# SSD scan: the norms' transposes and root broadcasts written to the four PSUM banks of the outputs' pool

## Chip, cores and metric

The kernel runs on one core of one Trainium2 chip. The metric is the device time of one execution in microseconds (us). Three executions of the kernel before gave 2980.72, 2979.49 and 2980.98 us, median 2980.72.

## What is computed

One step of a two-layer encoder on 1024 prompt frames and 64 sample frames (1088 columns). Layer 0 is an SSD (Mamba-2) mixer and a feed-forward block, layer 1 a chunk-band attention and a feed-forward block. The change is in layer 0's mixer. Cut to what matters:

```python
z, xbc, dt_raw = split(u @ w_in)                  # u = rmsnorm(x)
xs, Bm, Cm = split(silu(conv(xbc)))
y, h_final = ssd_scan(xs, softplus(dt_raw + dt_bias), -exp(A_log), Bm, Cm, h0)
y = (y + xs * D_skip) * silu(z)                   # (L, 2048)
yg = y.reshape(L, 4, 512)                         # 4 groups
yg = yg * rsqrt(mean(yg * yg, -1) + EPS)          # a norm for each group and row
return (yg.reshape(L, 2048) * gnorm_w) @ w_out
```

## The kernel before

Data lie with features on the 128 partitions and the 1088 columns along the free axis, in three slices of 384, 384 and 320 columns (`SL`, numbered s = 0, 1, 2). Matmuls of weights run in three passes each (lines 454 to 456: high part by high, high by low, low by high). Every tile that TensorE writes stands in one of the eight PSUM banks. In the SSD stage two belong to the pool `pmm` (tag `mm`, the projections), two to `pax` (tag `ax`, called the shared ones here) and four to `pyy` (tag `yy`).

**The stage.** TensorE's program is written by hand: the loop of lines 1079 to 1101 issues one projection tile after another (`unit`), and after each quarter or half of one `st.pump()` lets side tasks add their pieces, by due times on a clock that the program keeps for itself (`Stream`). The side tasks are

- `group_task`: two tiles `bnp`, `cbp` a slice and group, from `ax`;
- `ssd_task` for each block j of 128 features (16 of them, four to a group) and slice: a transpose `xtp` (line 866), read by VectorE as `xd` (876), and a state product `sp` (885), read by VectorE as `hn` (898), both from `ax`;
- `ssd_out` (809), once for two (j, s): two tiles `yp` and two tiles `yo` from `pyy`, read by VectorE at lines 830 and 832;
- at the end of a group's last block, for each slice, `rstd` (482): three transposes of the sums of squares `ssg` into `nst` (line 487), a reduce of it on VectorE (498) and eight small steps (499 to 511) that give the inverse roots `rst`;
- `build_y` (581): takes the finished y back from DRAM (`yt`, line 596), and for one column quarter q and group broadcasts the roots over the partitions, by two or three transposes into `nbp` (`bcast`, 517), which ScalarE copies to `rb` (520). `rb` has one buffer. VectorE multiplies (597), ScalarE and VectorE split the product into its high and low part (598, 599). This is the right-hand side of the output projection (`project`).

Before the change both `nst` and `nbp` came from `ax`, through the function of line 436. With two banks, a tile of `ax` has to wait until the tile two before it, or the one before it, has been read. Groups 0 to 2 have their three norms in the middle of the stage; the norms of group 3 stand in its last 15 us, mixed with the first broadcasts of `build_y`. That end is called the tail here.

**Order.** TensorE executes the program's order. The order on the other engines comes from a scheduler with priorities; `rstd` and the projections' evacuations have the highest (`HIP`). For the last block (j = 15) the sums of squares are added on VectorE (line 933, `end = V`) in place of GpSimd. From line 1104 on, the first output projection (`project`) runs, and then the feed-forward stage, whose pool `px0` takes over the four banks of `pyy`.

The program prints names without numbers: `nst<-ident,ssg` is a norm's transposes of this stage, `nst<-ident,ssum` one of another stage.

Of the kernel before, what the change touches and what calls it, by code (L numbers as in the profile page):

```python
# [8 lines left out]
F32 = mybir.dt.float32  # L9
# [7 lines left out]
P = 128  # L17
# [357 lines left out]
def hybrid_kernel(  # L375
# [57 lines left out]
    def col(c):  # L433
        return pcs[:, c:c + 1]

    def ax(name):
        return pax.tile([P, 512], F32, tag="ax", name=name)

    def mm(name):
# [21 lines left out]
    def unit(w, u, n, evac, parts=2, pl=None):  # L461
        ps_ = mm("mm") if pl is None else pl.tile([P, 512], F32, tag="mm", name="mmx")
        passes(ps_, w, lambda k: u[k], [(k, k) for k in range(KD)], n, parts=parts)
        evac(ps_)
        st.pump()
# [16 lines left out]
    def rstd(ssum, inv, r, nb, more=None):  # L482

        sp = ax("nst")
        if more is None:
            for i in range(nb):
                PE.transpose(sp[:, i * P:(i + 1) * P], ssum[:, i * P:(i + 1) * P], ident)
        else:
            for j, t in enumerate((ssum, more)):
                for i in range(nb):  # L490
                    c = 4 * j + i
                    PE.matmul(sp[:, c:c + 1], t[:, i * P:(i + 1) * P], ones[:, 0:1], start=True, stop=True)
        with tc.high_priority(HIP):
            v = nsb.tile([P, 12], F32, tag="nv", bufs=2, name="nv")
            a, h, y = v[:, 0:nb], v[:, 4:4 + nb], v[:, 8:8 + nb]
            if more is None:
                sums = sp[:, :nb * P].rearrange("p (a b) -> p a b", b=P)
                V.tensor_reduce(a, sums, axis=mybir.AxisListType.X, op=ALU.add)
                V.tensor_scalar(a, a, inv, EPS, op0=ALU.mult, op1=ALU.add)
            else:  # L500
                V.tensor_scalar(a, sp[:, :nb], inv, EPS, op0=ALU.mult, op1=ALU.add)
                V.scalar_tensor_tensor(a, sp[:, 4:4 + nb], inv, a, op0=ALU.mult, op1=ALU.add)
            V.tensor_scalar(y.bitcast(I32), a.bitcast(I32), -0.5, float(0x5F3759DF), op0=ALU.mult, op1=ALU.add)


            V.tensor_tensor(h, y, y, op=ALU.mult)
            V.tensor_tensor(h, h, a, op=ALU.mult)
            V.scalar_tensor_tensor(a, h, RP[0], h, op0=ALU.add, op1=ALU.mult)
            V.scalar_tensor_tensor(a, a, RP[1], h, op0=ALU.add, op1=ALU.mult)
            V.scalar_tensor_tensor(a, a, RP[2], h, op0=ALU.add, op1=ALU.mult)  # L510
            V.scalar_tensor_tensor(r, a, RP[3], y, op0=ALU.add, op1=ALU.mult)

    def bcast(r, a, n, rb=None):

        bp = ax("nbp")
        for i in range((a + n + P - 1) // P):
            PE.transpose(bp[:, i * P:(i + 1) * P], r[:, i:i + 1].to_broadcast([P, P]), ident)
        if rb is None:
            rb = nsb.tile([P, 384], F32, tag="rb", bufs=1, name="rb")
        A.activation(rb[:, :n], bp[:, a:a + n], AF.Copy, scale=RL)  # L520
        return rb[:, :n]
# [82 lines left out]
    def project(qs, uq, y, src, after=None, early=None, pl=None):  # L604


        ss = {}
        for mg in MGS:
            ws = early if early and mg is MGS[0] else [W.get() for _ in mg]
            for q in qs:  # L610
                n = QS[q][1]
                st.wait_for(lambda: q in uq)
                for m, w_ in zip(mg, ws):
                    ym = y[q][m // 4][:, m % 4, :]

                    def ev(ps):
                        with tc.high_priority(HIP):
                            if src is None:
                                A.copy(ym, ps[:, :n])
                            else:  # L620
                                V.tensor_tensor(ym, src[q][m // 4][:, m % 4, :], ps[:, :n], op=ALU.add)

                    if not (ws is early and q == qs[0]):
                        unit(w_, uq[q], n, ev, pl=pl)
                    if after:
                        if m == 0:
                            ss[q] = ssum_start(n)
                        add_sq(ss[q], ym, n, m == 0)
                    if q == qs[-1]:
                        W.put()  # L630
                if mg is MGS[-1]:
                    R.put(4)
                    if src is not None and src is not y:
                        R.put(2)
                    if after:
                        after(q, ss[q])

    with ExitStack() as es:
        pyy = es.enter_context(tc.tile_pool(reuse_waits="tile", name="pyy", bufs=4, space=PSUM))
# [34 lines left out]

        def table_task():
            ps = ax("dtn")
            for c in range(NCH):
                PE.matmul(ps[:, c * 32:(c + 1) * 32], dtT[c // 3][:64, (c % 3) * P:(c % 3 + 1) * P], stk, start=True, stop=True)
# [263 lines left out]
        def evac_of(kind, i):  # L942
            if kind == "z":
                def f(s, p_):
                    n = SL[s][1]
                    zst[i, s] = sb2.tile([P, 384], F32, tag="zs", bufs=3, name="zs")
                    scaled(zst[i, s][:, :n], p_, s, 0, n)
                    A.activation(zst[i, s][:, :n], zst[i, s][:, :n], AF.Silu)
                    if i == 15:
                        drop_u(s)  # L950
                        if s == 0:
                            st.spawn(build_y())
                return f
            if kind == "x":
                cvx = pair_t[i] = Conv(i, "xsT", 5)

                def f(s, p_):
                    cvx(s, p_)
                    st.spawn(ssd_task(i, s))
                return f  # L960
            if kind == "B":
                grp_t[i] = Conv(16 + i, "BT", 2), Conv(20 + i, "CT", 5)
                return grp_t[i][0]
            cvc = grp_t[i][1]

            def f(s, p_):
                cvc(s, p_)
                st.spawn(group_task(i, s), SSD_D)
            return f
# [71 lines left out]
        def scale_dt(s):  # L1041
            st.wait_for(lambda: s in done)
            ps = pend[s].pop(0)
            V.tensor_tensor(dtT[s][:64, :SL[s][1]], ps[:64, :SL[s][1]], rbs[s][:64, :SL[s][1]], op=ALU.mult)

        def finish(s):
            if s < 1:
                scale_dt(s)
            for e, ps in zip(ev, pend.pop(s)):
                e(s, ps)  # L1050

        for s in range(NSL):
# [23 lines left out]
                dps = dt_unit(us, n, pl, tg)  # L1076
            pend[s] = [dps] * (s < 2) + box
        finish(2)
        for grp in order:
            ws = [W.get() for _ in grp]  # L1080
            ev = [evac_of(*f) for f in grp]
            if len(grp) < 3:
                seq = [(i, s) for s in range(NSL) for i in range(len(grp))]
                if grp is order[0]:

                    seq = [(0, 0), (0, 1), (1, 0), (1, 1), (1, 2), (0, 2)]
            else:
                seq = [(0, 0), (1, 0), (0, 1), (0, 2), (2, 0), (1, 1), (2, 1), (1, 2), (2, 2)]
            for i, s in seq:
                kd_, jj_ = grp[i]  # L1090
                q = 3 * jj_ + s
                if kd_ == "x":
                    st.wait_for(lambda: so["C"] > q - 5)
                elif kd_ == "z":
                    st.wait_for(lambda: so["D"] > q - 3)
                elif kd_ == "C" and q >= 5:
                    g_, s_ = divmod(q - 5, 3)
                    st.wait_for(lambda: so["C"] > 3 * (4 * g_ + 3) + s_)
                unit(ws[i], u[s], SL[s][1], lambda p_: ev[i](s, p_))
                if s == 2:  # L1100
                    W.put()
# [5 lines left out]
            ya[q] = [v4(R.get(), QS[q][1]) for _ in range(2)]  # L1107
        project((0, 1), uy[0], ya, None)
        st.wait_for(lambda: so["D"] == 3 * XT and len(rst_done) == NG * NSL)


    class Ops:
# [889 lines left out]
```

## Time and profile before

| | |
|---|---|
| median of three executions | 2980.72 us |
| profiled execution | 2979.66 us, of which the span of its instructions is 2978.0 us |
| TensorE busy | 2921.0 us, 98% of the span |
| VectorE / ScalarE / GpSimd busy | 69% / 47% / 24% |
| SSD stage with group norms (200 to 640 us) | TensorE busy 434.56 of 440 us, VectorE 360.01 |
| tail (656 to 671 us) | TensorE busy 11.29 of 15 us, VectorE 15.00 |
| mean granted TensorE clock | 0.996 |

Times in the rows are us from the span's start. A row of the timeline has start, length, engine, line, operation, out<-in, shape and count, and in brackets how long the engine had been idle before it and what ended that. PE is TensorE's matmuls, DVE VectorE, ACT ScalarE, POOL GpSimd, SP the queue that issues DMAs. A matmul's end is modelled, and matmuls overlap: three transposes in a row are shown as 0.49 us, but the next instruction starts 0.32 us after the first of them. What one instruction costs the stream is therefore read from start to start. Each row of the waits says who waited for whom, the sum, how many times, and the longest.

### The profile page before, as it was taken

What the parts mean: (1) busy time and instruction counts of PE and PEld (TensorE: products, weight loads), DVE (VectorE), ACT (ScalarE), POOL (GpSimd) and SP (SyncE); (2) the same over time, 40 slices, a digit from 0 to 9 for tenths busy, and PEclk for the clock granted to TensorE, in tenths of its full rate; (3) what the DMA queues carried; (4) which work ended last, traced back from release to release, by engine and by line L of the source; (5) the groups of instructions that cost most, each with busy time, mean ns of one, the idle gap of its engine ahead of it and who ended that gap; (6) DMA issues with size and microseconds to landing.
All of it is one profiled execution on the core that took longest, in us unless ns stands there. A gap on an engine that the chain in (4) does not pass through costs nothing.

```text
span 2978.0 us, 56302 instructions
## 1 busy us (share of the span) xinstructions
PE 2921.0 (98%) x21626; PEld 2871.4 (96%) x21626; DVE 2040.2 (69%) x4471; ACT 1394.1 (47%) x2530; POOL 719.2 (24%) x821
## 2 busy tenths in 40 slices
PE   8999999999999999999999999999999999999999
PEld 7899999999999999999999899999999999999999
DVE  7887878885768545584567777777678645475544
ACT  6554646454453223344445665555653323244443
POOL 1333333331122343451111000000131343351111
PEclk9999999999999999999999999999999999999999
DMA  3333333244563222345665222223365222255654
GB/s 122 113 105 99 102 100 106 90 120 148 171 185 113 82 81 73 96 153 171 202 192 157 83 80 73 65 64 95 115 180 174 80 81 75 78 153 174 215 178 137
DMA packets 201551, 363.36 MB, mean 122 GB/s; under 512 B 20545, under 2 KB 149281, under 8 KB 201281
## 3 DMA queue, kind: packets, MB, share of 16 engines
q1 hardware_dynamic: 199488, 353.39, 38.6%
q0 software_dynamic: 1792, 6.36, 1.1%
q8 instruction: 170, 2.79, 0.4%
q14 instruction: 101, 0.82, 0.1%
HBM read 292.47 MB, written 62.74 MB: 119 GB/s over the span
## 4 chain that ended last, share of the span: by engine, by line
PE 83%; DVE 9%; DMA 3%; ACT 2%; issue 2%; POOL 0%; SPq 0%; DVEq 0%; ACTq 0%; POOLq 0%
PE px L1280 9%; PE px L1281 9%; PE px L1282 9%; PE mm L454 7%; PE mm L456 7%; PE mm L455 7%; PE po L1480 6%; PE po L1481 6%; PE po L1479 6%; PE mmx L455 3%; PE mmx L454 3%; PE mmx L456 3%; PE po L1763 2%; PE ptp L1724 1%; DVE sc L1702 1%
## 5 line engine op out<-in xcount | busy, mean ns | idle before, releaser
L454 PE MATMUL mm<-r,hl 128*128 128x384 f32 (+2 forms) x1664 | 555.2, 334 | 5.7 <-ACT BT L768 3.0
L456 PE MATMUL mm<-r,hl 128*128 128x384 f32 (+2 forms) x1664 | 539.0, 324 | 3.6 <-DVE hl L353 2.9
L455 PE MATMUL mm<-r,hl 128*128 128x384 f32 (+2 forms) x1664 | 537.8, 323 | 0.0
L341 DVE TENSOR_TENSOR hl<-raw,hl 128x1024 fp32r<-128x1024 f32 (+1 forms) x219 | 257.6, 1177 | 227.5 <-ACT hl L340 223.2
L1281 PE MATMUL px<-r,hl 128*128 128x288 f32 (+1 forms) x1184 | 347.3, 293 | 0.0
L454 PEld LDWEIGHTS mm<-r,hl 128*128 128x128 f32 x1664 | 314.7, 189 | 8.8 <-ACT BT L768 3.2
L456 PEld LDWEIGHTS mm<-r,hl 128*128 128x128 f32 x1664 | 313.9, 189 | 5.1 <-DVE hl L353 3.9
L455 PEld LDWEIGHTS mm<-r,hl 128*128 128x128 f32 x1664 | 315.0, 189 | 0.1
L1280 PE MATMUL px<-r,hl 128*128 128x288 f32 x1056 | 310.9, 294 | 0.0
L1282 PE MATMUL px<-r,hl 128*128 128x288 f32 x1056 | 310.7, 294 | 0.0
L340 ACT CAST hl<-raw 128x1024 fp32r<-128x1024 f32 (+1 forms) x219 | 219.9, 1005 | 176.1 <-PE po L1481 99.7
L480 POOL TENSOR_TENSOR ssum<-ssum,sq 128x256 f32<-128x256 f32 (+3 forms) x97 | 129.2, 1333 | 639.6 <-ACT sq L479 624.3
L1281 PEld LDWEIGHTS px<-r,hl 128*128 128x128 f32 x1184 | 222.3, 188 | 0.0
L1282 PE MATMUL px<-rx,hl 128*128 128x256 f32 x768 | 214.9, 280 | 6.6 <-DVE hl L341 6.6
L1280 PE MATMUL px<-rx,hl 128*128 128x256 f32 x768 | 215.4, 280 | 0.8 <-ACT hl L340 0.8
L1480 PE MATMUL po<-rx,hl 128*128 128x384 f32 (+1 forms) x624 | 201.5, 323 | 0.2 <-DVE rx L1344 0.2
L1280 PEld LDWEIGHTS px<-r,hl 128*128 128x128 f32 x1056 | 198.4, 188 | 0.2 <-DVE u L1295 0.2
L1282 PEld LDWEIGHTS px<-r,hl 128*128 128x128 f32 x1056 | 198.3, 188 | 0.0
L1479 PE MATMUL po<-rx,hl 128*128 128x384 f32 (+1 forms) x608 | 197.3, 324 | 0.0
L1481 PE MATMUL po<-rx,hl 128*128 128x384 f32 (+1 forms) x608 | 196.5, 323 | 0.0
L1281 PE MATMUL px<-rx,hl 128*128 128x256 f32 x640 | 178.7, 279 | 0.0
L290 POOL TENSOR_TENSOR tt<-raw 128x512 f32<-128x512 f32 x40 | 55.4, 1386 | 438.3 <-DMA raw<-in_w_f_dram 333.9
(359 smaller groups left out, 8052.6 us busy)
## 6 DMA issues: line engine op xcount, KB each, us to landing
raw<-in_w_f_dram SPq DMA_DIRECT2D x154, 512.0 KB, 3.8
rx<-in_w_f_dram SPq DMA_DIRECT2D x54, 512.0 KB, 3.7
raw<-in_w_in_dram SPq DMA_DIRECT2D x40, 512.0 KB, 3.6
MT<-ascr SPq DMA_DIRECT2D x48, 384.0 KB, 4.3
sg<-hscr SPq DMA_DIRECT2D x88, 192.0 KB, 3.5
raw<-in_w_f_dram SPq DMA_DIRECT2D x44, 384.0 KB, 3.4
raw<-in_w_so_dram SPq DMA_DIRECT2D x32, 512.0 KB, 4.0
raw<-in_w_kv_dram SPq DMA_DIRECT2D x18, 512.0 KB, 3.5
```

Source lines behind the costliest of these rows:

```text
L340: self.nc.scalar.copy(h, v)
L341: (eng or self.eng or self.nc.vector).tensor_tensor(lo, v, h, op=ALU.subtract)
L454: PE.matmul(ps[:, :n], h_, xh, start=(first and i == 0), stop=False)
L455: PE.matmul(ps[:, :n], h_, xl, start=False, stop=False)
L456: PE.matmul(ps[:, :n], l_, xh, start=False, stop=(last and i == nk - 1))
L480: (eng or G).tensor_tensor(ssum[:, :n], ssum[:, :n], q[:, :n], op=ALU.add)
L1280: PE.matmul(ps, wh, ah[:, k, :], start=(k == 0), stop=False)
L1281: PE.matmul(ps, wh, al[:, k, :], start=False, stop=False)
L1282: PE.matmul(ps, wl, ah[:, k, :], start=False, stop=(k == 3))
L1479: PE.matmul(ps[:, :n], wh, xh, start=(k == 0), stop=False)
L1480: PE.matmul(ps[:, :n], wh, xl, start=False, stop=False)
L1481: PE.matmul(ps[:, :n], wl, xh, start=False, stop=(k == FT - 1))
```

## The change

From the end of the stage's opening (after `finish(2)`) to the end of the first output projection, `ax` hands the tiles named `nst` and `nbp` out of `pyy`, tag `yy`. All other tiles stay where they were. No instruction is added or taken away.

```diff
+    side = [None]
+
     def ax(name):
+        if side[0] and name in ("nst", "nbp"):
+            return side[0].tile([P, 512], F32, tag="yy", name=name)
         return pax.tile([P, 512], F32, tag="ax", name=name)
...
         finish(2)
+        side[0] = pyy
         for grp in order:
...
         project((0, 1), uy[0], ya, None)
         st.wait_for(lambda: so["D"] == 3 * XT and len(rst_done) == NG * NSL)
+        side[0] = None
```

Lines behind the edits have numbers higher by 2 (from line 436), 4 (from 437), 5 (from 1079) and 6 (from 1110). The order on TensorE and GpSimd stays as it was. What changes on TensorE is which instruction waits for whom. First the norm of a group's last slice, before: the transposes of the sums, between a state product and the next block's transpose ("..." stands for the further transposes of the same tile).

```order
L816 MATMUL yp<-MT,xd 64x128 x12
L826 MATMUL yo<-CT,hn 128x128 x4
L826 MATMUL yo<-CT,hn 128x128 [waits DVE_49]
L885 MATMUL sp<-xe,Bn 128x128 [waits Pool_49]
...
L487 MATMUL nst<-ident,ssg 128x128 [waits DVE_49]
...
L866 MATMUL xtp<-ident,xsT 128x128 [waits DVE_49,Activation_49]
```

The same place with the change.

```order
L820 MATMUL yp<-MT,xd 64x128 x12
L830 MATMUL yo<-CT,hn 128x128 x2
L830 MATMUL yo<-CT,hn 128x128 [waits DVE_49]
...
L889 MATMUL sp<-xe,Bn 128x128 [waits Pool_49]
...
L491 MATMUL nst<-ident,ssg 128x128 [waits DVE_49]
...
L870 MATMUL xtp<-ident,xsT 128x128 [waits Activation_49]
```

`xtp` no longer waits for VectorE: before, that wait was for the reduce of `nst`, whose bank it took. `nst` itself still waits for VectorE, now for the read of the `yp` of the output pass above, whose bank it takes.

The second place is TensorE in the tail, behind the last output pass of the stage. Before:

```order
L826 MATMUL yo<-CT,hn 128x128 [waits DVE_49]
L826 MATMUL yo<-CT,h_7532 128x64 [waits DMAHW3_49]
L517 MATMUL nbp<-ident,rst 128x128 [waits Activation_49]
...
L487 MATMUL nst<-ident,ssg 128x128 [waits DVE_49]
...
L454 MATMUL mm<-r,hl 128x256
```

With the change:

```order
L830 MATMUL yo<-CT,hn 128x128 [waits DVE_49]
L830 MATMUL yo<-CT,h_7532 128x64 [waits DMAHW3_49]
L521 MATMUL nbp<-ident,rst 128x128 [waits DVE_49]
...
L491 MATMUL nst<-ident,ssg 128x128 [waits DVE_49]
...
L458 MATMUL mm<-r,hl 128x256
```

`nbp` waited for ScalarE's copy of the broadcast before it; now it waits for VectorE's read of this pass's first `yp` (line 830, now 834). `nst` waited for its sums; now it waits for VectorE's read of this pass's first `yo` (line 832, now 836). Behind them stands the next projection.

The third place is VectorE in the tail, from its read of that `yp` to the last sums of squares (line 933, now 937, 320 columns). Before (rows left out at "..."):

```order
L830 SCALAR_TENSOR_TENSOR y<-xsT,pcs,yp 128x384
L498 TENSOR_REDUCE nv<-nst 128x3
L832 TENSOR_TENSOR ea<-yo,ea 128x384
L499 TENSOR_SCALAR nv<-nv 128x3
L830 SCALAR_TENSOR_TENSOR y<-xsT,pcs,yp 128x320
...
L341 TENSOR_TENSOR hl<-raw,hl 128x1024
L498 TENSOR_REDUCE nv<-nst 128x3
L933 TENSOR_TENSOR ssg<-ssg,sq 128x320
```

With the change:

```order
L834 SCALAR_TENSOR_TENSOR y<-xsT,pcs,yp 128x384
L836 TENSOR_TENSOR ea<-yo,ea 128x384
L834 SCALAR_TENSOR_TENSOR y<-xsT,pcs,yp 128x320
L836 TENSOR_TENSOR ea<-yo,ea 128x320
L502 TENSOR_REDUCE nv<-nst 128x3
...
L341 TENSOR_TENSOR hl<-raw,hl 128x1024
L937 TENSOR_TENSOR ssg<-ssg,sq 128x320
L603 TENSOR_TENSOR r<-yt,r 128x256
L502 TENSOR_REDUCE nv<-nst 128x3 x2
```

The four reads of the output pass now stand together ahead of the first reduce, and the second slice's reduce has moved behind the last sums. On ScalarE a few casts and copies change places in the tail. On SP one load of a weight (`raw<-in_w_so_dram`) now stands ahead of two loads of `yt` that it stood behind.

## The prediction

> **What bounds the kernel now.** I read the busy times of the page first, then the busy time by stage, then TensorE's waits in the stretch that the change touches, and then the timelines of the places where it waits.
>
> ```profile
> span 2978.0 us, 56302 instructions
> PE 2921.0 (98%) x21626; PEld 2871.4 (96%) x21626; DVE 2040.2 (69%) x4471; ACT 1394.1 (47%) x2530; POOL 719.2 (24%) x821
> ```
>
> TensorE is busy for 98% of the span, so time goes where TensorE stands still or where its clock is low. The stages differ, though. In the table by stage the columns are the stretch, its length, the busy time of PE, PEld, DVE, ACT and POOL (with counts), the granted clock, and the DMA engines' share and rate.
>
> ```profile
> 200.00:640.00 440.00, 434.56 (x3066) 425.12 (x3065) 360.01 (x922) 232.31 (x357) 162.98 (x266) 1.00 0.32 100
> 640.00:656.00 16.00, 14.52 (x97) 14.03 (x96) 15.07 (x36) 7.72 (x18) 5.98 (x7) 1.00 0.36 105
> 656.00:671.00 15.00, 11.29 (x104) 10.40 (x103) 15.00 (x43) 6.43 (x15) 2.61 (x3) 1.00 0.51 150
> 671.00:720.00 49.00, 49.00 (x399) 49.00 (x398) 21.74 (x47) 19.56 (x39) 0.00 (x0) 0.97 0.39 117
> ```
>
> From 200 to 640 us, with the norms of groups 0 to 2, TensorE is the bound: 434.56 of 440 us against VectorE's 360.01. From 656 to 671 us, the tail, it is the other way round: VectorE is busy for all of 15.00 us and TensorE for 11.29. After that TensorE has no gap to 720 us and VectorE is under half busy. So an idle microsecond of TensorE is worth a microsecond in the first and last of these stretches, and nothing in the tail, unless VectorE gets through sooner too.
>
> ```profile
> PE xtp L866 <- DVE nv L498: 4.8, 6, 0.8
> PE nst L487 <- DVE nv L499: 2.7, 1, 2.7
> PE nbp L517 <- DVE nv L498: 0.8, 1, 0.8
> PE sp L885 <- ACT rb L520: 0.8, 1, 0.8
> PE nbp L517 <- DVE hn L898: 0.7, 1, 0.7
> ```
>
> These are TensorE's waits from 200 to 700 us, but for two smaller ones. The first row is the change's target: six times a block's transpose waits 0.8 us for the reduce of the norm just issued. The other four lie in the tail.
>
> **Groups 0 to 2: the gain.** Below is TensorE in group 0: the norms of the first, second and last slice, and last an `xtp` and `sp` with no norm ahead, for comparison.
>
> ```profile
> 231.29 0.83 PE L885 MATMUL sp<-xe,Bn 128*128 128x128 f32 x6
> 232.20 0.52 PE L866 MATMUL xtp<-ident,xsT 128*128 128x128 f32 x3
> ...
> 240.93 0.49 PE L487 MATMUL nst<-ident,ssg 128*128 128x128 f32 x3
> 242.22 0.52 PE L866 MATMUL xtp<-ident,xsT 128*128 128x128 f32 x3 [0.80 <-DVE nv L498]
> ...
> 250.21 0.49 PE L487 MATMUL nst<-ident,ssg 128*128 128x128 f32 x3
> 251.49 0.52 PE L866 MATMUL xtp<-ident,xsT 128*128 128x128 f32 x3 [0.80 <-DVE nv L498]
> ...
> 624.36 0.49 PE L866 MATMUL xtp<-ident,xsT 128*128 128x128 f32 x3
> 624.68 0.83 PE L885 MATMUL sp<-xe,Bn 128*128 128x128 f32 x6
> 625.27 0.39 PE L454 MATMUL mm<-r,hl 128*128 128x320 f32 x1
> ```
>
> From start to start three transposes take 0.32 us (624.36 to 624.68) where nothing waits, and 1.29 and 1.28 where the next tile waits for the reduce: 0.97 and 0.96 lost. In the first slice the product stands between the two; it takes 0.91 (231.29 to 232.20) against 0.59 (624.68 to 625.27): 0.32 lost. Together 2.25 us a group. The waits' row has six waits of one size, two a group, so three groups give **6.75 us**. With the change the six `xtp` have no wait for VectorE's reduce left, as the built order shows.
>
> Does the rest keep up? VectorE waits for TensorE in this stage, not the other way.
>
> ```profile
> DVE craw L721 <- PE mm L456: 20.4, 11, 3.0
> 247.78 1.27 DVE L830 SCALAR_TENSOR_TENSOR y<-xsT,pcs,yp 128x384 f32<-128x384 f32 x2 [0.26 <-PE yp L816]
> ```
>
> Eleven waits, 20.4 us, are VectorE's for one kind of projection alone; it has 80 us free in 440. So it moves along with TensorE. The price in the new home is a wait of `nst` for the reads of `yp`: in the last slice these two reads end at 249.05 (247.78 + 1.27), and `nst` starts at 250.21, 1.16 us later. VectorE had waited for that very `yp` (0.26), so the reads move with TensorE and the cover stays; were it gone, it would cost less than the 0.97 that is won there. Price: 0, at most 0.3 a group.
>
> **The tail: little.** TensorE, and below it VectorE.
>
> ```profile
> 659.19 0.39 PE L517 MATMUL nbp<-ident,rst 128*128 128x128 f32 x2
> 659.41 0.49 PE L487 MATMUL nst<-ident,ssg 128*128 128x128 f32 x3
> 666.08 0.52 PE L487 MATMUL nst<-ident,ssg 128*128 128x128 f32 x3 [0.23 <-DVE rst L511]
> 669.29 0.52 PE L487 MATMUL nst<-ident,ssg 128*128 128x128 f32 x3 [2.69 <-DVE nv L499]
> 670.60 0.46 PE L517 MATMUL nbp<-ident,rst 128*128 128x128 f32 x2 [0.80 <-DVE nv L498]
> ...
> 659.79 0.60 DVE L830 SCALAR_TENSOR_TENSOR y<-xsT,pcs,yp 128x384 f32<-128x384 f32 x1
> 660.79 0.54 DVE L832 TENSOR_TENSOR ea<-yo,ea 128x384 f32<-128x384 f32 x1
> 668.20 0.54 DVE L498 TENSOR_REDUCE nv<-nst 128x3 f32<-128x384 f32 x1
> 668.67 0.47 DVE L933 TENSOR_TENSOR ssg<-ssg,sq 128x320 f32<-128x320 f32 x1
> ```
>
> The two waits of 0.8 (`sp`) and 0.7 (`nbp`) before 656 us go: both were for banks. TensorE then reaches the `nbp` of 659.19 about 6.75 + 1.5 = 8.3 us earlier, near 650.9, and meets the **new wait**: VectorE's read of `yp`, which ended at 660.39, comes only 6.75 us earlier, since VectorE has no idle time here: 653.6. So TensorE stands for some 2.7 us at `nbp`, and `nst` behind it for 0.4 more until the read of `yo`. Queued behind both is the projection, with some 6.7 us of work (659.41 to 666.08) until the next `nst`. The 1.5 us are lost again, and TensorE's lead is back at that of VectorE.
>
> What ends the tail is the last slice's `nst` at 669.29. The profile names the reduce's second step, but its data, the sums of line 933, end at 669.14, and these stay. VectorE gets to them one reduce sooner (668.20 to 668.67), because the order puts it behind: **0.47 us**. The last `nbp` waited for that norm's reduce, 1.31 us from start to start; in another bank it follows after 0.32: **0.99 us**. Here TensorE is again the bound. Sum so far: 6.75 + 0.47 + 0.99 = 8.2 us.
>
> What else moves is covered. On SP a weight load passes two loads of `yt`, which in the profile were issued at 677.91 for a broadcast that TensorE has at 711.25; a load takes 4.0 us to land.
>
> ```profile
> 677.91 0.80 SPq L596 DMA_DIRECT2D yt<-yscr  x2
> 711.25 0.38 PE L517 MATMUL nbp<-ident,rst 128*128 128x128 f32 x2
> raw<-in_w_so_dram SPq DMA_DIRECT2D x32, 512.0 KB, 4.0
> ```
>
> That is 33 us of cover for a delay of a few. ScalarE's exchanged casts stand where it is busy for 6.43 of 15 us. Both cost 0; without their cover, a cast or a load, 0.4 to 4 us.
>
> **The clock.** The same table, in steps of 3.41 us that end where the granted clock changes (the last figure but two):
>
> ```profile
> 667.47:670.88 3.41, 0.79 (x6) 0.59 (x7) 3.41 (x12) 1.09 (x4) 0.00 (x0) 1.00 0.64 216
> 670.88:674.30 3.42, 3.42 (x19) 3.42 (x18) 3.42 (x20) 1.22 (x3) 0.00 (x0) 0.50 0.51 143
> 937.12:940.54 3.42, 1.04 (x7) 0.64 (x5) 3.32 (x3) 2.30 (x4) 0.00 (x0) 1.00 0.79 233
> 940.54:943.95 3.41, 3.14 (x14) 3.14 (x15) 2.99 (x4) 2.77 (x4) 2.66 (x2) 0.50 0.16 53
> 2295.63:2299.04 3.41, 1.84 (x17) 1.65 (x15) 3.41 (x5) 0.00 (x0) 0.00 (x0) 1.00 0.70 219
> 2299.04:2302.46 3.42, 2.50 (x21) 2.50 (x22) 2.54 (x4) 1.88 (x3) 1.76 (x2) 1.00 0.30 112
> ```
>
> After a step with 0.79 or 1.04 us of work the next one runs at 0.50; after 1.84 us it does not. The two waits that end the tail (2.69 and 0.80) so cost another half of 3.42, 1.7 us, right where TensorE is the bound again. With the change the idle time moves forward, to 650.9 to 654. A low step after that falls on the projection ahead of the last `nst`. Unthrottled, TensorE would be there about 1.2 us early (653.6 + 0.4 + 6.7 = 660.7 against 669.14 - 6.75 - 0.47 = 661.9), so of 1.7 us lost, at most 0.5 gets through; I take 0.3. The stretch behind the tail keeps its full clock: 1.7 - 0.3 = **1.4 us**. [...]
>
> **Sum.** 8.2 + 1.4 = 9.6 us off the profiled execution's own 2979.66 us (1.66 us lie outside its span): 2970.1. The median shown, 2980.72, is 1.06 above that execution, so I predict 2971.1. Under 0.2%, 6.0 us, a difference can't be told from none.
>
> **Rivals.**
>
> - *The clock goes against it.* Every later pair of waits is moved by some 9 us against the steps of 3.41, and may fall into one step, as at 937.12, or be split over two, as at 2295.63; the low step that is won in the tail may come back behind it. For: both cases are in the rows. Against: the moves can as well save the step at 940.54. Each step is worth 1.7 us; with the tail's not won and one more lost, 2970.1 + 1.4 + 1.7, or 2974.3 as a median. Chance 0.17.
> - *VectorE doesn't follow.* If in groups 0 to 2 the next evacuation comes no sooner, TensorE waits there for what it had won, and half of the 6.75 is left, with the tail's terms as they are: 2974.5; with none but the first slice's and half of the tail's, 2978. For: VectorE is 82% busy. Against: its 20.4 us of waiting for TensorE. Chance 0.14.
> - *Slower: the output banks hold up the broadcasts.* At the tail's `nbp` TensorE waits for a VectorE that is full; the projection and the later broadcasts queue behind it. It costs only what exceeds VectorE's own pace: the break-even is a read of `yp` some 9.6 us later than the 660.39 of the profile. If each of the tail's five tiles from 659.19 on waited for VectorE for as long as the worst there now (2.69), 13.5 us would be lost for 8.2 won: 2986. Against: the reads now stand first on VectorE. Chance 0.04.
> - *It does nothing*, because another wait stands behind the one removed: 2980.7. The comparison rows have `xtp` with no idle time ahead. Chance 0.03.
>
> **How the numbers follow.** The forecast has 0.62. Its own range is 2968 to 2974: one step of the clock more or less is 1.7, VectorE's pace in the tail 1. With the two milder rivals 2967.5 to 2976 leaves out less than 2 in 10. Faster by over 0.2% (under 2974.8): the forecast, two thirds of the first rival and some of the second, 0.78; same 0.17; slower 0.05.
>
> **What would show it.** In the waits of 200 to 700 us the row of `xtp` for line 498's reduce is gone, and three groups end 6.75 us sooner (the `xtp` at 624.36 stands near 617.6). In the tail a new row has `nbp` waiting 2 to 4 us for the `y` of line 834, and the last `nst` still waits for VectorE. The low clock step comes ahead of the last `nst`, not behind it. If `xtp` waits for another name, or the lead shrinks between 250 and 640 us, the first term is wrong; if `nbp` doesn't wait, VectorE wasn't the tail's bound.

## The result and the profile after

| | before | after |
|---|---|---|
| median (lowest to highest), 9 runs each | 2981.37 us (2979.49 to 2983.44) | 2971.86 us (2969.44 to 2976.22) |
| profiled execution / its span | 2979.66 / 2978.0 us | 2969.44 / 2967.7 us |
| ratio of the times, 95% interval | | 0.997 (0.9961 to 0.9979) |

The change takes 9.5 us off the median, 0.3%. The forecast was 2971.1 us, 9.6 us less than before. First the page of the changed kernel, and TensorE's waits in it from 200 to 700 us.

```profile
PE 2918.9 (98%) x21626; PEld 2872.6 (97%) x21626; DVE 2039.9 (69%) x4471; ACT 1394.2 (47%) x2530; POOL 715.4 (24%) x821
```

```profile
PE nbp L521 <- DVE y L834: 3.0, 1, 3.0
```

Every wait of before is gone from this stretch, the six of `xtp` among them, and one new one has come: `nbp`, which now waits 3.0 us for VectorE's read of `yp`. The busy times of the engines are almost those of before; what went is idle time of TensorE. The table by stage, with its borders moved by 6.75 to 8 us (200 to 633 is the stage with the group norms, 649 to 664 the tail), says the same. Its columns are those of the prediction's table; the granted clock is the last figure but two.

```profile
200.00:633.25 433.25, 433.20 (x3071) 425.77 (x3070) 359.99 (x922) 232.59 (x357) 163.10 (x267) 1.00 0.32 101
...
649.00:664.00 15.00, 11.95 (x89) 11.57 (x87) 14.02 (x48) 5.48 (x14) 1.83 (x2) 0.89 0.48 155
664.00:712.00 48.00, 48.00 (x404) 48.00 (x403) 22.68 (x45) 21.50 (x43) 0.63 (x1) 1.00 0.43 136
```

TensorE stood still for 5.44 us of 440 before and stands still for 0.05 of 433.25 now. In the tail it still stands for 3.05 us of 15; the low clock (0.89) has moved in there, and the stretch behind has its full clock (1.00, before 0.97). The low clock is one step of 3.41 us (653.39 to 656.80) with a granted clock of 0.50; such a step is called a half step below.

### The profile page after: what moved, and what is told of

Its sections match the earlier page's. It is cut to its first block, busy times and chain, and to the rows that moved or that the text cites. A ratio compares the mean times of both kernels' runs of the same rounds, so it can differ in the third digit from the quotient of the medians.

```text
span 2967.7 us, 56306 instructions
## 1 busy us (share of the span) xinstructions
PE 2918.9 (98%) x21626; PEld 2872.6 (97%) x21626; DVE 2039.9 (69%) x4471; ACT 1394.2 (47%) x2530; POOL 715.4 (24%) x821
## 3 DMA queue, kind: packets, MB, share of 16 engines
q8 instruction: 170, 2.79, 0.4%
## 4 chain that ended last, share of the span: by engine, by line
PE 83%; DVE 9%; DMA 3%; ACT 2%; issue 2%; POOL 0%; SPq 0%; DVEq 0%; ACTq 0%; POOLq 0%
PE px L1286 9%; PE px L1287 9%; PE px L1288 9%; PE mm L458 7%; PE mm L460 7%; PE mm L459 7%; PE po L1486 6%; PE po L1487 5%; PE po L1485 5%; PE mmx L459 3%; PE mmx L458 3%; PE mmx L460 3%; PE po L1769 2%; DVE sc L1708 1%; PE ptp L1730 1%
```

## Experiments

Totals of one kernel spread by 2 to 10 us from run to run, so each total below is set against runs of the kernel before on the same chip, and beside it stands what the trace says by place. For that I take the start of the same TensorE instruction in two traces, the kernel's and that of before, and look how the difference grows between four places: 200 us, 630 us (the groups' norms are done), 675 us (the tail is done), 2960 us (the end), all in the time of before. A minus is time won.

| kernel | median, change against before on that chip | groups, 200 to 630 | tail, 630 to 675 | rest, 675 to 2960 |
|---|---|---|---|---|
| whole change | 2971.86, -9.5 | -7.50 | -2.73 | +0.45 |
| whole change, once more | 2971.81, -8.9 | -5.66 | -1.74 | +1.22 |
| 1 groups 0 to 2 alone | 2973.86, -8.4 | -7.49 | +0.23 | +2.40 |
| 2 tail alone | 2980.03, -2.2 | -0.42 | -2.56 | +2.38 |
| 3 `nst` alone | 2968.40, -13.9 | -7.38 | -3.54 | +0.46 |
| 3 `nst` alone, once more | 2969.78, -10.9 | -7.12 | -3.50 | +0.62 |
| 4 whole, idle spot filled | 2972.94, -9.3 | -6.90 | -3.23 | +0.84 |
| 5 before, idle spot filled | 2982.27, +0.7 | +0.07 | -1.29 | +2.54 |
| 6 groups alone, priority | 2973.67, -7.9 | -6.98 | -0.74 | +1.16 |
| 7 `nst` alone, priority | 2970.58, -11.0 | -7.58 | -3.48 | +0.18 |
| 8 as 7, fill in the next stage | 2974.30, -7.3 | -7.47 | -3.38 | +5.08 |
| 9 as 3, fill in the next stage | 2969.65, -11.0 | -7.55 | -3.53 | +0.21 |

The last column is positive everywhere: the profiled execution of before, 2979.66, was itself below the medians of before on these chips (2980.68 to 2982.25). Another part are half steps: from 680 us on before has two (940.54 and 1688.06 us), kernels 1 and 2 have two each near 930 us alone (930.85 and 934.26; 936.75 and 940.16). Kernel 5 loses 2.0 us near 1540 us, where TensorE's waits are 1.2 us against 0.2 before. Kernels 2 and 5 change nothing in the groups and show -0.42 and +0.07 there: so much the place by place figures vary by themselves.

A kernel with other banks or more matmuls is also scheduled anew. Against before, VectorE's order differs in kernel 1 in nine places, all at the groups' norms; against the changed kernel, kernels 3 and 4 have over thirty instructions of VectorE's in the tail in other places. So those differences in the tail are those of the edit and of the new order together.

**1, the groups alone.** Only the `nst` of groups 0 to 2 move:

```diff
+                side[0] = pyy if g < 3 else None
                 rstd(ssg[:, s * 384:(s + 1) * 384], 1.0 / 512, rst[:, 3 * s:3 * s + 3, g], 3)
+                side[0] = None
```

> Only the norms' transposes (nst) of groups 0 to 2 take the outputs' banks; group 3's nst and all broadcasts nbp stay in the two shared banks, so the tail keeps the order of before. My theory (the six waits of xtp for the reduce were 2.25 us a group, and TensorE is the bound there): 6.75 to 7.5 us less than before, about 2974; the row of xtp waiting for the reduce is gone; in the tail the two waits of 2.7 and 0.8 us at the last nst and nbp are back, and the half-clock step behind them. Rival 1 (the change's gain is mostly the clock's and the tail's): 0 to 2 us less. Rival 2 (VectorE doesn't keep up in the groups): about 3 less, with new waits of TensorE for VectorE between 250 and 640 us.

Measured: ratio 0.998 (0.9971 to 0.999), and in the groups -7.49, the whole change's -7.50. In the tail the old waits are back, as TensorE's waits of this kernel from 200 to 700 us show.

```profile
PE nst L491 <- DVE nv L503: 2.7, 1, 2.7
...
PE nbp L521 <- DVE nv L502: 0.8, 1, 0.8
```

So the first term of the sum is shown, and both rivals (0 to 2 us, 3 us) fall: VectorE does follow.

**2, the tail alone.** The `nst` of group 3 and all `nbp` move, the `nst` of groups 0 to 2 don't:

```diff
+                keep = side[0]
+                side[0] = keep if g == 3 else None
                 rstd(ssg[:, s * 384:(s + 1) * 384], 1.0 / 512, rst[:, 3 * s:3 * s + 3, g], 3)
+                side[0] = keep
```

> The other half alone: group 3's nst and all nbp take the outputs' banks, the nst of groups 0 to 2 stay in the shared ones. My theory: the six waits of 0.8 us at xtp stay, the groups end when they did before; the tail gives 0.5 (a reduce less ahead of the last sums) + 1.0 (last nbp) + about 1.2 (the half-clock step moves ahead of the last nst) = 2.7 us less than before, about 2978.5. Together with the first half that makes the whole change, so the two halves add up to 9.5 to 10. Rival (the new wait of nbp for the read of y, 3.0 us, is a cost of its own): 0 to 2 us more than before. Rival (the gain in the groups shrinks the tail's, or the other way): the two halves add up to 2 us more or less than the whole.

Measured: ratio 0.9993 (0.9984 to 1.0001), which by itself doesn't tell 2.7 from nothing. The trace does: its waits are the two rows below, and the tail gives -2.56 in spite of the 3.2.

```profile
PE xtp L870 <- DVE nv L502: 4.8, 6, 0.8
PE nbp L521 <- DVE y L834: 3.2, 1, 3.2
```

The two halves add up to -10.6 in the medians, where the whole change has -9.5 and -8.9, and to -7.49 - 0.42 + 0.23 - 2.56 = -10.24 in the traces, where the whole has -10.23 and, once more, -7.40: within the spread they don't eat each other's gain. The new wait isn't a cost of its 3.2 us.

**3, without the new wait.** All `nst` move, `nbp` stays:

```diff
-        if side[0] and name in ("nst", "nbp"):
+        if side[0] and name == "nst":
```

> All nst take the outputs' banks, the broadcasts nbp stay in the shared ones: the new wait of nbp for the read of y (3.02 us) is taken away by another bank. In the built order the first nst of group 3 now waits for that read instead, and nbp in the tail for ScalarE's and VectorE's reads as before. My theory (the wait is worth nothing by itself, it only holds TensorE at VectorE's pace; what it costs is the half-clock step behind it): the idle time moves a few instructions on, total within 1 us of the whole change, at best 0.8 less if no half-clock step follows. Rival 1 (the new wait is a cost of 3.0 us): 2 to 3 us less than the whole change, about 2969. Rival 2 (moving nbp was where the tail's gain came from): 1 to 2.7 more than the whole change.

> All nst in the outputs' banks, all nbp in the shared ones, once more, beside the whole change on one chip. My theory (moving nbp made the 3.02 us wait, which costs only the half-clock step that follows it, 0.8 us at the last nst): 0.8 to 1.4 us less than the whole change, 10.5 to 12 less than before. Rival (the first lead of 3.5 us was real): 3 us less than the whole change. Rival (it was chance): the same as the whole change.

The second time it ran beside the whole change, whose expectation was:

> The whole change once more, unchanged, as the neighbour on the same chip for the next two kernels. My theory (6.75 to 7.5 us in the groups, 2.7 in the tail): 9 to 10.5 us less than before, about 2972; the half-clock step ahead of the last nst and the 3.0 us wait of nbp are there again. Rival (part of the first result was chance): under 8 us less.

The table below is TensorE's waits of this kernel, first run.

```profile
PE nst L491 <- DVE ssg L937: 0.9, 1, 0.9
PE nst L491 <- DVE y L834: 0.9, 1, 0.9
PE sp L889 <- ACT rb L524: 0.8, 1, 0.8
PE nbp L521 <- DVE hn L902: 0.7, 1, 0.7
```

The 3.0 us wait is gone, four smaller ones stand for 3.3 us, and the granted clock is 1.00 from 652 to 659 us, in the second run too. The tail gives -3.54 and -3.50 against -2.73: 0.8 more, as forecast, where the rival had 3. The totals put it 2.0 us below the whole change on one chip (2969.78 of 5 runs, 2969.01 to 2971.09, and 2971.81 of 8 runs, 2967.73 to 2974.45) and, by the changes against before, 4.3 across chips (-13.9 and -9.5 in the table); of this the tails account for 0.8 in the first pair of traces, and for 1.8 in the second, where the whole change had two half steps in its tail. That the rest is more than spread isn't shown. Against before it is 0.9963 (0.995 to 0.9975) and 0.9966 (0.9953 to 0.9978). It beats both kernels, the changed one by 0.8 to 1.8 us in the tails of the traces.

In that second run of the whole change the groups gave only 5.66: TensorE waited 1.0 us there once for a projection's evacuation (`craw`), which in the other traces is 0.3 at most, and the tail's half-clock step came twice in a row (652.39 and 655.80 us, both 0.50).

**4, work put into the new wait.** Ahead of the waiting `nbp`:

```diff
+                if (q, g) == (1, 1):
+                    fill = ax("fill")
+                    for _ in range(12):
+                        PE.matmul(fill[:, :P], ones, ones, start=True, stop=True)
```

> The whole change, plus twelve matmuls of 128x128 that nobody reads (about 1.3 us of work by the 0.32 us of three transposes), put in a shared bank ahead of the nbp that waits 3.02 us for the read of y: extra work in an idle spot. My theory (the half-clock step behind the wait comes from the little work in the step before it, and gets through to the last nst by about 0.8 us): the step behind 653 us runs at full clock, the last nst starts right behind the last sums, total 0.5 to 1 us less than the whole change. Rival (only the wait counts, the low clock is covered by VectorE): no change, or up to 1.3 us more if the matmuls don't fit into the wait. [...]

Measured: no difference in the total (2972.94, ratio 0.9972, 0.9963 to 0.9981), since the expected 0.5 to 1 us lies below what totals tell. First the steps of the clock around the wait in the changed kernel, then in this one (the second figure is the busy time of PE, the last but two the granted clock).

```profile
649.98:653.39 3.41, 0.81 (x6) 0.57 (x6) 3.41 (x10) 1.80 (x5) 0.36 (x1) 1.00 0.66 211
653.39:656.80 3.41, 3.41 (x18) 3.41 (x17) 3.41 (x12) 1.20 (x4) 1.48 (x2) 0.50 0.20 66
```

```profile
651.59:655.00 3.41, 3.10 (x27) 2.67 (x26) 3.41 (x10) 1.52 (x4) 0.32 (x1) 1.00 0.85 249
655.00:658.42 3.42, 3.42 (x31) 3.42 (x30) 3.15 (x5) 0.80 (x2) 1.53 (x2) 1.00 0.35 118
```

With 3.10 us of work in the step in place of 0.81, the half step is gone, and the tail gives 0.50 us more (-3.23 for -2.73). The twelve matmuls took not 1.3 us but 2.90 (their row, 651.01 us), and still cost nothing: TensorE had that time to spare. The 0.50 isn't the price of the half step alone, because VectorE's new order here puts the last sums later:

```profile
661.71 0.49 DVE L941 TENSOR_TENSOR ssg<-ssg,sq 128x320 f32<-128x320 f32 x1
...
662.26 0.55 PE L491 MATMUL nst<-ident,ssg 128*128 128x128 f32 x3 [0.78 <-DVE ssg L941]
```

At 630 us this trace is 1.64 us behind that of the changed kernel (-6.28 and -7.92). The sums end at 662.20, or 660.56 in that kernel's time, where they end at 660.06: 0.50 later. The last `nst` now waits 0.78 us for them, as expected, and still starts 0.55 sooner (662.26 - 1.64 against 661.17). So the half step, not the wait, is what the new place of `nbp` costs, 0.5 us at the least; with the changed kernel's own sums it comes to about 1.0, as the part on the tail below works out.

**5, the same in the kernel before**, in the wait of 2.69 us at the end of its tail:

```diff
+                if (g, s) == (3, 2):
+                    fill = pyy.tile([P, 512], F32, tag="yy", name="fill")
+                    for _ in range(12):
+                        PE.matmul(fill[:, :P], ones, ones, start=True, stop=True)
```

> The kernel before, plus twelve matmuls of 128x128 that nobody reads (about 1.3 us), into a bank of the outputs' pool ahead of the last slice's nst of group 3, that is into the 2.69 us wait that ends the tail. My theory (that wait leaves 0.79 us of work in a step of 3.41 us, so the next step runs at half clock, and TensorE is the bound there): no half step at 671 to 674, everything behind it 1.7 us sooner relative to the start of the tail, total 1.7 us less than before, about 2979.5. [...] Rival (the work costs more than it saves): up to 1.3 us more.

Its trace around the fill, and the two steps of the clock from there:

```profile
665.80 2.84 PE L939 MATMUL fill<-ones 128*128 128x128 f32 x24
...
670.15 0.43 PE L517 MATMUL nbp<-ident,rst 128*128 128x128 f32 x2 [0.98 <-ACT rb L520]
```

```profile
666.27:669.68 3.41, 2.90 (x25) 2.49 (x23) 3.34 (x10) 1.24 (x4) 0.00 (x0) 1.00 0.55 168
669.68:673.09 3.41, 2.94 (x25) 2.94 (x26) 3.37 (x16) 1.55 (x5) 0.00 (x0) 1.00 0.50 153
```

The half step is gone (it stood at 670.88 with 0.79 us of work ahead of it), and TensorE is 1.29 us sooner behind the tail; 1.5 of the 1.7 come behind that `nbp`, as in the changed kernel, and 0.2 are lost ahead of it, where it waits 0.18 us longer than before. The stretch of the kernel before that lies where this step lies (666.90 to 670.31 us) has 0.52 us of work without the fill, against 2.90 us here. The total didn't move (1.0001, 0.9992 to 1.0009): the interval holds the 1.7 us as well as nothing, and in the trace the 2.0 us lost near 1540 us, where TensorE's waits are 1.2 us against 0.2 before, undo it. In the trace the clock did what I expected; as a gain of the whole kernel it isn't shown here.

**6, the bank or VectorE's order?** Kernel 1 and a high priority for what leads to the last sums:

```diff
+            with tc.high_priority(HIP if j == XT - 1 else 0):
                 end.tensor_tensor(y[:, :n], y[:, :n], zst[j, s][:, :n], op=ALU.mult)
...
+                with tc.high_priority(HIP if j == XT - 1 else 0):
                     A.activation(sq[:, :n], y[:, :n], AF.Square)
                     end.tensor_tensor(ssg[:, o:o + n], ssg[:, o:o + n], sq[:, :n], op=ALU.add)
```

> The nst of groups 0 to 2 in the outputs' banks, group 3's nst and all nbp in the shared ones (the tail's banks as before), and a high priority on VectorE and ScalarE for the last block's three products with z, squares and sums, so that VectorE gets to them sooner. My theory (the tail ends with VectorE's last sums, and what it does ahead of them is what counts, not the bank of nbp): against the same kernel without the priority the wait of 2.69 us at the last nst shrinks to about that of a reduce (1 us), the half step behind it goes, 2 to 3.5 us less, in all 9 to 11 less than before. Rival (the sums wait for ScalarE's squares or for the z products' data, not for VectorE's order): no change against the kernel without the priority, about 7.3 less than before.

Here my theory failed. Ratio 0.9975 (0.9965 to 0.9985), 7.9 us less than before and no better than kernel 1 (0.998, 0.9971 to 0.999). In the tail the trace has -0.74 against kernel 1's +0.23, so 1.0 of the expected 2 to 3.5 us. Measured from 630 us, the last sums come 2.6 us sooner on VectorE than in kernel 1, but the last `nst` only 0.9. VectorE, then TensorE:

```profile
661.15 0.48 DVE L939 TENSOR_TENSOR ssg<-ssg,sq 128x320 f32<-128x320 f32 x1
...
662.83 0.54 DVE L502 TENSOR_REDUCE nv<-nst 128x3 f32<-128x384 f32 x1
```

```profile
663.43 0.55 PE L491 MATMUL nst<-ident,ssg 128*128 128x128 f32 x3 [2.38 <-DVE nv L502]
```

The sums are there at 661.63 (661.15 + 0.48), the `nst` starts at 663.43, behind the reduce that frees its bank (662.83 + 0.54 = 663.37). In the shared banks the reduce is a second bound, 1.7 us behind the first, and the half step behind the tail stays (from 666 us a matmul is shown with 0.41 us where it had 0.28). In the kernel before both ended within 0.4 us (reduce 668.74, sums 669.14), so its trace couldn't tell them apart.

**7, both.** The diff of 3 and of 6 together.

> All nst in the outputs' banks, all nbp in the shared ones, and the high priority for the last block's z products, squares and sums. My theory (VectorE's last sums end the tail): the 0.95 us wait of the last nst for the sums goes, about 1 us less than the same kernel without the priority, in the tail (200 to 675 us) 11.5 to 12.5 us less than before in all, total about 2967.5. Rival (ScalarE's squares or the reads of y end the tail): no change by the priority. Rival (the priority pushes other evacuations back): 1 to 3 us more, with a new wait of TensorE for a projection's evacuation.

Measured: 0.9959 (0.9946 to 0.9971), the tail -3.48, the same as kernel 3: the expected 1 us didn't come. The wait of the last `nst` for the sums is gone; in its place the last `nbp` waits 1.0 us for `rst`, its own data, the result of the eight small steps.

```profile
661.05 0.82 PE L491 MATMUL nst<-ident,ssg 128*128 128x128 f32 x6
...
662.88 0.40 PE L521 MATMUL nbp<-ident,rst 128*128 128x128 f32 x2 [1.01 <-DVE rst L515]
```

The priority has pulled the sums ahead of those steps, and VectorE needs the same time for both. In these runs neither the bank nor this order had anything left to give on that path; VectorE's work there would be next.

**8 and 9, the half step of the next stage.** The traces of before, of the changed kernel and of kernels 1, 2 and 3 have one or two half steps near 930 us (0.50 from 940.54, 929.87, 930.85, 936.75 and 929.08 us), in kernel 3 behind waits of 0.65 and 1.9 us for weights. In 8 (kernel 7 with twelve unread matmuls in `run_pair`) I put the fill one product too late, behind the waits:

> The kernel with all nst in the outputs' banks, nbp in the shared ones and the priority, and twelve more matmuls of 128x128 that nobody reads in the feed-forward stage, where TensorE waits 0.65 and 1.9 us for weights ahead of the first products at about 928 us. In all traces so far a step with about 1.0 us of work there is followed by one or two at half clock. My theory (it is the little work in one step of 3.41 us that brings the half step): no half step at 929 to 936 us, 1.7 us less than the kernel without the fill (3.4 where that one has two such steps). Rival (the low clock follows from the stage's load): the half step stays.

Measured: 2974.30, 3.7 us more than kernel 7; the half step at 931 stays (0.87 us of work ahead of it), and the fill stands on the path: from 930 to 950 us the kernel falls 2.4 us behind kernel 7. That is what such work costs where TensorE has no idle time, for comparison with 4 and 5. In 9 (kernel 3, six matmuls) it stands between the waits:

```diff
                 PE.matmul(ps, wh, al[:, k, :], start=False, stop=False)
+                if hd is hd_[0] and (t_, b, p_, k) == (NB0, 0, P6, 0):
+                    fill = ax("fill")
+                    for _ in range(6):
+                        PE.matmul(fill[:, :P], ones, ones, start=True, stop=True)
                 PE.matmul(ps, wl, ah[:, k, :], start=False, stop=(k == 3))
```

> All nst in the outputs' banks, nbp in the shared ones, without the priority, and six unread matmuls of 128x128 (1.4 us, by the 2.84 us that twelve took in the tail) in the feed-forward stage, this time one product earlier than in the fill that came too late: behind the two matmuls that stand between the waits of 0.65 and 1.9 us at about 928 us. My theory (little work in one step of 3.41 us brings the half step): the step there has about 2.4 us of work, no half step follows at 929 to 933, and from there on 1.7 us is won against the same kernel without the fill. Rival (the threshold is higher, or the load decides): the half step stays, no gain. A difference of 1.7 in totals is near what the spread of runs lets one see; the list of low steps and the starts in the trace decide.

The clock steps of this kernel there, and the longest of TensorE's waits from 925 to 960 us:

```profile
927.08:930.49 3.41, 2.19 (x18) 1.80 (x16) 3.31 (x4) 1.97 (x2) 0.00 (x0) 1.00 0.78 198
930.49:933.90 3.41, 3.41 (x30) 3.41 (x31) 2.98 (x4) 2.89 (x4) 2.97 (x2) 1.00 0.14 47
```

```profile
PE px L1286 <- DVE u L1305: 2.4, 1, 2.4
```

No half step follows, and from 675 to 945 us 1.63 us is won against before, which has its half step there (-10.19 to -11.82; the same steps in kernel 3's second trace: 0.85 us of work, then a half step, and -10.70 to -10.50). But this row is new: a product at 938 us now waits 2.4 us for VectorE's read of a tile, because VectorE took a long operation ahead of that read:

```profile
935.55 2.45 DVE L1160 TENSOR_TENSOR r<-r 128x1152 fp32r<-128x1152 f32 x1
937.92 0.41 DVE L1305 TENSOR_TENSOR u<-px,p 128x256 f32<-128x256 f32 x1
```

In kernel 3, whose lines have numbers lower by 4 there, the read stands first (second trace):

```profile
935.24 0.41 DVE L1301 TENSOR_TENSOR u<-px,p 128x256 f32<-128x256 f32 x1
...
936.97 1.35 DVE L1160 TENSOR_TENSOR r<-r 128x1152 fp32r<-128x1152 f32 x1
```

These two and one between them are the only instructions of VectorE's whose order the fill changed; ScalarE's and GpSimd's order is the same. So the loss comes with the new order. By 1300 us the difference is back to -9.83. The total is that of kernel 3 (2969.65 and 2969.78).

## Why the prediction was right

**Groups 0 to 2: 6.75 forecast, 7.50 in the trace.** In group 0 of the changed kernel TensorE runs the norm and the next block without a pause.

```profile
230.54 0.49 PE L491 MATMUL nst<-ident,ssg 128*128 128x128 f32 x3
230.87 0.83 PE L889 MATMUL sp<-xe,Bn 128*128 128x128 f32 x6
231.54 0.49 PE L870 MATMUL xtp<-ident,xsT 128*128 128x128 f32 x3
...
240.23 0.49 PE L491 MATMUL nst<-ident,ssg 128*128 128x128 f32 x3
240.56 0.49 PE L870 MATMUL xtp<-ident,xsT 128*128 128x128 f32 x3
...
248.50 0.49 PE L491 MATMUL nst<-ident,ssg 128*128 128x128 f32 x3
248.82 0.49 PE L870 MATMUL xtp<-ident,xsT 128*128 128x128 f32 x3
```

From `nst` to `xtp` it takes 0.33 and 0.32 us where it took 1.29 and 1.28: the terms 0.96 and 0.97. In the first slice the product takes 0.67 (230.87 to 231.54) where it took 0.91: 0.24 for the 0.32 forecast. Read across its three norms alone, each group gives 2.27 to 2.29 us, 6.84 for the three, against 2.25 each; and it does so in every one of the ten traces in which these `nst` moved, also in the one with 5.66. What differs between traces lies elsewhere, at the first matmul of a projection. Of the 0.66 beyond 6.84 here, 0.27 came at the one of 362.03 and 0.38 at this one, both of the kernel before:

```profile
515.98 0.41 PE L454 MATMUL mm<-r,hl 128*128 128x384 f32 x1 [0.33 <-DVE craw L721]
```

That was a wait for an evacuation; in kernel 2, which leaves the groups alone, it went too (0.35). So the mechanism and its size were right, and nothing here shows that the extra 0.66 is the change's. The price in the new home is 0, as taken: no `nst` waits in a group. The `xtp` of 624.36 stands at 616.43, 7.9 us sooner, of which 0.4 were there at 200 us.

That VectorE follows was argued from its waits for TensorE. They went down by most of what TensorE gained:

```profile
DVE craw L725 <- PE mm L460: 17.4, 10, 3.0
...
DVE zs L725 <- PE mm L460: 5.3, 9, 0.7
```

`craw` had 20.4 us before, and `zs` 8.2 us: 5.9 us less in the two, of VectorE's 80 us free.

**The tail: 1.46 and 1.4 forecast, 2.73 in the trace: the sum right, two sizes in it off.** TensorE and VectorE of the changed kernel:

```profile
652.54 0.43 PE L521 MATMUL nbp<-ident,rst 128*128 128x128 f32 x2 [3.02 <-DVE y L834]
...
661.17 0.49 PE L491 MATMUL nst<-ident,ssg 128*128 128x128 f32 x3
661.50 0.38 PE L521 MATMUL nbp<-ident,rst 128*128 128x128 f32 x2
```

```profile
651.89 0.60 DVE L834 SCALAR_TENSOR_TENSOR y<-xsT,pcs,yp 128x384 f32<-128x384 f32 x1
...
659.58 0.48 DVE L937 TENSOR_TENSOR ssg<-ssg,sq 128x320 f32<-128x320 f32 x1
...
661.38 1.02 DVE L502 TENSOR_REDUCE nv<-nst 128x3 f32<-128x384 f32 x2 [0.98 <-PE nst L491]
```

- *The new wait*: 2.7 forecast, 3.02 measured, at the tile and for the read named. That it costs nothing by itself, only holds TensorE at VectorE's pace, is shown by 2, 3 and 4.
- *The last sums* came 1.17 us sooner than the groups' gain alone would have them (668.67 to 659.58 is 9.09, less 7.92), not 0.47. One reduce less ahead of them is 0.47; the rest is two of the small steps, 0.66 and 0.83 us long before, for 0.15 each now, less one multiplication (`yt`) that went from 0.47 to 0.95: 0.51 + 0.68 - 0.48 = 0.71. Before:

```profile
661.78 0.66 DVE L503 TENSOR_SCALAR nv<-nv 128x3 int32<-128x3 int32 x1
...
663.22 0.83 DVE L507 TENSOR_TENSOR nv<-nv 128x3 f32<-128x3 f32 x1
```

- *The half step ahead of the last `nst`* was sized at 0.3 and is about 1.0: the last sums end at 660.06, the last slice's `nst` starts at 661.17, 1.11 behind them, where before had 0.15, so 0.96. Kernel 4 agrees: 0.50 won without the half step, with sums 0.50 later. So the sentence that the last `nst` still waits for VectorE was wrong: TensorE arrives last, and VectorE waits 0.98 us for the first of the two `nst` that stand there. For the most part the two wrong sizes are one error: the forecast let VectorE's sums cover the half step, and sums that come 0.70 sooner cover 0.70 less. That is why they nearly cancel: 1.17 - 0.96 = 0.21, and `nst` moved by 0.22 more than the groups' 7.92, against 0.47 - 0.3 = 0.17 forecast.
- *The last `nbp`* no longer waits for the reduce: 0.99 forecast, 1.01 measured (its shift less that of `nst`, 9.15 - 8.14).
- *The half step behind the tail* is gone: 1.5 from there to 675 us (10.65 - 9.15), 1.7 forecast. In kernel 1, which keeps the tail's old order, it stands at 661.19, with 0.70 us of work ahead of it.

The three parts make 0.22 + 1.01 + 1.5 = 2.73, against 0.17 + 0.99 + 1.7 forecast.

**What was luck.** The total came out within 0.1 us of the forecast (9.5 and 9.6), which is closer than anything here can be told: single runs of a kernel spread by 2 to 10 us, and the second measurement of the whole change has -8.9 in the median and -7.40 by 675 us in its trace. The terms at the norms and at the last `nbp` are met by their mechanism; the sum of the tail is met because one error in it counts twice, with opposite signs.

**The rivals.** That the clock goes against it: it did in single executions (two half steps in the tail of the second run, two at 930 us in kernels 1 and 2), but not on the median. That VectorE doesn't follow: refuted by 1. That the output banks hold up the broadcasts: the wait is there, 3.0 us, once and not five times; the reads standing first on VectorE, which was the argument against this rival, is what the traces show. What the forecast didn't see is that keeping `nbp` where it was would have been better still (kernel 3): of the two tiles only `nst` had a wait that cost time.

## What to carry to other kernels

A wait for a bank is worth its length only in a stage where the waiting engine is the bound: six waits of 0.8 us in the groups, with what went along, gave 6.84 us, while 3 us more of waiting in the tail cost 0.5 to 1.0 us, through the clock. When a tile is given another bank, ask for each tile by itself which read it waits for then and which engine is full there, and move only those that gain. Where two releasers end at the same time, as the reduce and the sums here, taking away one gains only up to the other: both have to go.

When an edit lets the scheduler order another engine anew, compare that engine's order in the two traces before a gain or a loss is put down to the edit: kernels 4 and 9 each won at the clock and lost at VectorE's new order.

## What the runs showed of the hardware

**Where the half clock came.** From 200 to 2960 us each of the traces of before and of the changed kernel has three stretches with a granted clock of 0.50, each 3.41 us long: from 670.88, 940.54 and 1688.06 us in before, from 653.39, 929.87 and 1677.39 us in the changed kernel. In the 3.41 us ahead of them TensorE works 0.79, 1.04 and 1.22 us, and 0.81, 1.02 and 1.45 us. Kernels 4, 5 and 9 added matmuls to such a step: work went from 0.81 to 3.10, from 0.79 to 2.90 and from 0.85 (kernel 3's second run) to 2.19 us, and the step behind has 1.00. The added matmuls change the work in a step and its idle time together, so these runs don't show which of the two it goes by; that it is the work was my estimate from the rows. A half step can be followed by another. This is kernel 1 near 930 us:

```profile
927.44:930.85 3.41, 1.31 (x10) 0.90 (x8) 3.31 (x4) 2.64 (x4) 0.00 (x0) 1.00 0.83 243
930.85:934.26 3.41, 2.79 (x13) 2.79 (x14) 3.06 (x4) 2.49 (x3) 2.38 (x2) 0.50 0.21 72
934.26:937.67 3.41, 3.41 (x18) 3.41 (x18) 3.41 (x4) 0.40 (x2) 3.41 (x2) 0.50 0.01 3
937.67:941.08 3.41, 3.41 (x31) 3.41 (x31) 3.31 (x6) 0.42 (x1) 0.13 (x1) 1.00 0.55 159
```

Behind the half step with 2.79 us of work came a second one, and behind that one, with 3.41 us, the clock was 1.00 again.

Little work isn't what all half steps have ahead of them. In the kernel's opening a step that is busy from end to end is also followed by one. This is the kernel before there, and what fills 2.19 us of that step:

```profile
53.07:56.48 3.41, 3.41 (x27) 3.17 (x26) 1.45 (x4) 1.81 (x2) 0.10 (x1) 1.00 0.00 0
56.48:59.89 3.41, 3.41 (x15) 3.41 (x14) 1.48 (x5) 1.72 (x3) 0.46 (x2) 0.50 0.00 0
```

```profile
53.55 2.19 PE L678 MATMUL dtn<-stk,dtT 64*128 64x32 f32 x18
```

In the changed kernel it is the same: 3.41 us of work from 52.65 us, the same eighteen matmuls in 2.19 us of it, and 0.50 from 56.06 us. Why the clock falls there isn't shown.

**Half steps make a part of the spread.** Of the 3.41 us of one, 1.5 were won behind the tail in the changed kernel and 1.6 in kernel 9, where TensorE is the bound, and their number differs between executions of one kernel: the second run of the whole change has two in its tail (652.39 and 655.80 us) for one (653.39 us). The slowest of the changed kernel's nine runs (2976.22) has a mean clock of 0.994, the fastest (2969.44) 0.996; that half steps make most of the spread isn't shown, and kernel 5 loses 2.0 us near 1540 us, where its waits are 1.2 us against 0.2. And removing one isn't yet a gain: in kernel 9 the 1.6 us won were lost 5 us later to VectorE's new order.
